# Two small tiles lengthened: where the operands of an encoder layer's products begin in a partition

## The chip, the core and the metric

The kernel runs on one core of one Trainium2 chip. The metric is the device time of one execution in microseconds (us), the median of several runs.

## What is computed

One layer of a bidirectional encoder, 256 tokens of 2048 features in float32: a half-step SwiGLU, a mixer with four neighbourhood heads and twelve dilated heads over one q/k/v projection, a second half-step SwiGLU, and a gated per-layer embedding. Each sublayer stands between two RMS norms.

```python
f = _swiglu(_rmsnorm(h, ffn1_pre_g[i]), ffn1_w_gate[i], ffn1_w_up[i], ffn1_w_down[i])
h = h + 0.5 * _rmsnorm(f, ffn1_post_g[i])
m = _mixer(_rmsnorm(h, mix_pre_g[i]), w_qkv[i], na_rpb[i], out_g[i], w_o[i])
h = h + _rmsnorm(m, mix_post_g[i])
f = _swiglu(_rmsnorm(h, ffn2_pre_g[i]), ffn2_w_gate[i], ffn2_w_up[i], ffn2_w_down[i])
h = h + 0.5 * _rmsnorm(f, ffn2_post_g[i])
g = jax.nn.sigmoid(_rmsnorm(h, ple_pre_g[i]) @ w_ple_gate[i])
h = h + _rmsnorm(g * (p[i] @ w_ple_proj[i]), ple_post_g[i])
```

The weight matrices are 2048 x 5632 (gate and up of both SwiGLUs, and their transposed shape for down), 2048 x 6144 (q/k/v), 2048 x 2048 twice (output and embedding gate) and 256 x 2048 (embedding projection).

## The kernel before

**The products.** `product` (L89) multiplies the activations of both token tiles (128 tokens each) with a block of 512 columns of a weight matrix. A float32 operand is split into two float32r parts, high and low, and three matmuls (L114, L115, L116) stand for one: high by high, low by high, high by low. In each of them the activation tile, 128 x 128, is the stationary operand, which TensorE loads by a LDWEIGHTS of its own, and the weight tile, 128 x 512, is the moving one. A name in the profile such as `down<-wh,hid_h` reads: result, moving operand, stationary operand. With three matmuls for each weight tile of 128 x 512 and each of two token tiles, the whole layer has 8304 of these matmuls.

**Stationary operands.** The normalised input of a sublayer lies in the tiles `u_h` and `u_l` of the pool `acts`; gate, up, q, k, v and the embedding gate (`pg`) read them. The embedding's own input `p_h`, `p_l` lies in the pool `work` (`pp` reads it). The hidden values of a SwiGLU and the heads' outputs lie in `hid_h` and `hid_l`, in pools that are opened behind all others (`ffn1`, `mix`, `ffn2`); down and the output projection (`mo`) read them.

**Moving operands.** `load_pairs` (L61) brings four row tiles of a weight into `raw` (three buffers) by one DMA of the SP queue, ScalarE writes the high part `wh` (L74 or L79), VectorE the low part `wl` (L75 or L80), seven buffers of two row tiles each, all in the pool `wpool`.

**Other work of TensorE.** Between the products stand transposes (L150, L353, L406), the scores (L391) and the weighted sums (L412) of the attention, all in plain float32.

**Where tiles lie.** Pools take up a partition one behind the other, in the order in which they are opened (L43 to L49), and a tile's length in bytes is rounded up to a multiple of 32. `mhalf` (L57) is the exponent -0.5 of the norms' power; it lies in the first pool, `const`, ahead of `h`, `acts`, `wpool`, `gpool` and `work`. `r` (L135) is the norm's factor, one float a token, in 16 buffers of the pool `small`, which is the last of the pools opened at the start; `ffn1`, `mix` and `ffn2` begin behind it. The order of the instructions is that of the program's text.

Of the kernel before, what the change touches and what calls it, by code (L numbers as in the profile page):

```python
# [15 lines left out]
P = 128  # L16
# [9 lines left out]
EPS = 1e-6  # L26
# [5 lines left out]

@with_exitstack
def encoder_layer(ctx: ExitStack, tc: tile.TileContext, a: dict, out: bass.AP):
    """One layer, 256 tokens in two tiles of 128 partitions.

    A float32 operand of a large product is split exactly into two float32r parts (12 bits of
    significand each); high x high + low x high + high x low are accumulated in PSUM. The weights
    stream through once, as the moving operand, for both token tiles.
    """  # L40
    nc = tc.nc

    const = ctx.enter_context(tc.tile_pool(name="const", bufs=1))  # L43
# [7 lines left out]
    ps_tr = ctx.enter_context(tc.tile_pool(name="ps_tr", bufs=2, space=PSUM))  # L51
    ps_o = ctx.enter_context(tc.tile_pool(name="ps_o", bufs=2, space=PSUM))

# [1 line left out]
    ident = const.tile([P, P], F32, name="ident")  # L55
    make_identity(nc, ident)
    mhalf = const.tile([P, 8], F32, name="mhalf")  # L57
    nc.gpsimd.memset(mhalf, -0.5)

# [1 line left out]
    def load_pairs(w, r0, nk, c0, g):  # L61
        """Split parts of w[r0 : r0 + nk * 128, c0 : c0 + 512], two row tiles at a time; with g,
        of the rows times the gain of their feature."""
        pairs = []
        for k0 in range(0, nk, 4):
            n = min(4, nk - k0)
            raw = wpool.tile([P, 4, NB], F32, name="raw", bufs=3)
            rows_ = w[r0 + k0 * P : r0 + (k0 + n) * P, c0 : c0 + NB]
            raw_loads.append(nc.sync.dma_start(raw[:, :n], rows_.rearrange("(k p) n -> p k n", p=P)))
            for j in range(0, n, 2):  # L70
                wh = wpool.tile([P, 2, NB], F32R, name="wh", bufs=7)
                wl = wpool.tile([P, 2, NB], F32R, name="wl", bufs=7)
                if g is None:
                    nc.scalar.copy(wh, raw[:, j : j + 2])  # L74
                    nc.vector.tensor_tensor(wl, raw[:, j : j + 2], wh.bitcast(F32), op=ALU.subtract)  # L75
                else:
                    for i in range(min(2, n - j)):
                        k = r0 // P + k0 + j + i
                        nc.scalar.activation(wh[:, i], raw[:, j + i], AF.Copy, scale=g[:, k : k + 1])  # L79
                        nc.vector.scalar_tensor_tensor(  # L80
                            wl[:, i], raw[:, j + i], g[:, k : k + 1], wh[:, i].bitcast(F32),
                            op0=ALU.mult, op1=ALU.subtract,
                        )
                pairs.append((wh, wl))
        return pairs
# [3 lines left out]
    def product(  # L89
        acc, lhs, w, r0, c0, g=None, first=True, last=True, steps=None, ahead=None, mid=None, jobs=True  # L90
    ):
        """acc[t] += lhs.T @ w[r0 : r0 + len(lhs) * 128, c0 : c0 + 512] for both token tiles.

        lhs[k] is (high, low), each [128, 256]. The row tiles of w are taken in steps (of SUPER
        at the most), each for one token tile and then the other, so that the first is done ahead
        of the second. ahead() comes before each step; with jobs, what waits in later comes behind
        the first; mid() comes where MID row tiles are left, of the second token tile.
        """
        nk = len(lhs)
        s0 = 0  # L100
        for n in steps or [nk % SUPER] * (nk % SUPER > 0) + [SUPER] * (nk // SUPER):
            if ahead is not None:
                ahead(s0)
            pairs = load_pairs(w, r0 + s0 * P, n, c0, g)
            for t in range(NT):
                tok = slice(t * P, (t + 1) * P)
                for k in range(n):
                    if mid is not None and t == NT - 1 and s0 + n == nk and k == n - MID:
                        mid()
                    wh, wl = pairs[k // 2]  # L110
                    xh, xl = lhs[s0 + k]
                    lead = first and s0 + k == 0
                    tail = last and s0 + k == nk - 1
                    nc.tensor.matmul(acc[t], xh[:, tok], wh[:, k % 2], start=lead, stop=False)  # L114
                    nc.tensor.matmul(acc[t], xl[:, tok], wh[:, k % 2], start=False, stop=False)  # L115
                    nc.tensor.matmul(acc[t], xh[:, tok], wl[:, k % 2], start=False, stop=tail)  # L116
            s0 += n
            if jobs:
                for job in later:
                    job()  # L120
                later.clear()
# [2 lines left out]
        return [ps_acc.tile([P, NB], F32, name=f"{name}{t}", tag="acc") for t in range(NT)]  # L124

    def gain(g, c0, name):
        """g[c0 : c0 + 512] in every partition."""
        t = gpool.tile([P, NB], F32, name=name, tag="gain")
        nc.sync.dma_start(t, bass.AP(tensor=g.tensor, offset=g.offset + c0, ap=[[0, P], [1, NB]]))
        return t  # L130

    def rsqrt_mean(v, n, scale):
        """v holds n partial sums of squares a token; 1 / (scale * sqrt(mean + EPS))."""
        m = small.tile([P, 1], F32, name="m")
        r = small.tile([P, 1], F32, name="r", bufs=16)  # L135
        c = scale * scale
        nc.vector.tensor_reduce(m, v, axis=AX.X, op=ALU.add)
        nc.gpsimd.tensor_scalar(m, m, c / n, c * EPS, op0=ALU.mult, op1=ALU.add)
# [5 lines left out]
        nc.scalar.activation(sq, x, AF.Square, accum_out=acc_col)  # L144

    def transposed_split(x, hi, lo, t):
        """x [128 tokens, 512] -> hi, lo [128, 4, 256], their columns of token tile t."""
        tr = ps_tr.tile([P, KB, P], F32, name="tr", tag="tr")
        for k in range(KB):
            nc.tensor.transpose(tr[:, k], x[:, k * P : (k + 1) * P], ident)  # L150
# [9 lines left out]
    def rows(blocks):  # L160
        return [(hi[:, k], lo[:, k]) for hi, lo in blocks for k in range(KB)]

# [1 line left out]
    h = resid.tile([P, NT, D], F32, name="h")  # L164

    # Gains of the features that go into a product, which are in the partitions of the weights:
    # of the four sublayers' inputs, and of the heads.
    row_g = const.tile([P, 5, D // P], F32, name="row_g")
    nc.sync.dma_start(row_g, a["row_gT"].rearrange("p (i k) -> p i k", i=5))

    # First input, from x with features in the partitions: loaded two row tiles at a time, between
    # those of the first weights.
    xT = a["xT"].rearrange("(k p) s -> p k s", p=P)
    x_blocks = [new_split(acts, "u", D // NB) for _ in range(D // NB)]

# [20 lines left out]
        return rsqrt_mean(ss, D, 1.0)  # L196

    def residual(fg, ssf, scale, blocks, rs):
        """h += fg / (scale * rms), transposed and split into blocks; and its pre-norm factor a
        token, which is applied behind the product and worked out behind its first part. A  # L200
        generator that stops after each half of a token tile; the first half needs fg[0] only."""
        blocks += [new_split(acts, "u", D // NB) for _ in range(D // NB)]
        r = []
        for b0 in range(0, D // NB, 2):
# [72 lines left out]
                down_out(1)  # L277
            f0 += ng

# [1 line left out]
    with tc.tile_pool(name="ffn1", bufs=2) as pool:  # L281
        f = pool.tile([P, NT, D], F32, name="f", bufs=1)
        ssf, u_blocks, u_rs = square_sums(), [], []
# [5 lines left out]
        list(res)  # L289
    rs = u_rs  # L290

# [1 line left out]
    mix = ctx.enter_context(ExitStack())  # L293
    pool = mix.enter_context(tc.tile_pool(name="mix", bufs=1))
    with ExitStack() as att:
        mconst = att.enter_context(tc.tile_pool(name="mconst", bufs=1))
        attn = att.enter_context(tc.tile_pool(name="attn", bufs=1))

        # Additive bias, queries in the partitions: [128, query tile, (head,) 256 keys].
        dil_bias = mconst.tile([P, NT, S], F32, name="dil_bias")  # L300
        nc.sync.dma_start(dil_bias, a["dil_bias"].rearrange("(t p) k -> p t k", p=P))
        na_mask = attn.tile([P, NT, S], F32, name="na_mask", tag="y", bufs=2)
        nc.sync.dma_start(na_mask, a["na_mask"].rearrange("(t p) k -> p t k", p=P))
        # In the place of the last heads' output.
        na_bias = [
            pool.tile([P, KB, S], F32, name="na_bias", tag=f"hid_{x}", bufs=4) for x in "hl"
        ]
        # Row q - k of the position bias: loaded with each grid row's queries in reverse, where it
        # is a window that moves by one a partition, and put in order by a permutation.
        flip = mconst.tile([P, P], F32, name="flip")  # L310
        nc.sync.dma_start(flip, a["flip"])
        rpb = a["rpb_pad"]
# [31 lines left out]
        later.append(query_factor)  # L344

        def heads_transposed(acc, fac, rotate, name):
            """[128, 4 heads, 256 tokens] of a projection, scaled and rotated."""
            xT_ = attn.tile([P, KB, S], F32, name=name)

            def turn(y, t):  # L350
# [27 lines left out]
            return xT_  # L378

        def attend(qT, kT, v, bias, o_split):  # L380
            """Four heads of softmax(q k + bias) v, normalised a head, transposed and split."""
            for t in range(NT):
                tok = slice(t * P, (t + 1) * P)
                o = ps_o.tile([P, KB, HD], F32, name="o")
# [50 lines left out]
        for g in range(4):  # L435
# [14 lines left out]
                nc.scalar.activation(v[:, t], acc[t], AF.Copy, scale=rs[t])  # L450
            o_split = new_split(pool, "hid", 4)
            if g == 0:
                bias = lambda t, hh: na_bias[t][:, hh]  # noqa: E731
            else:
                bias = lambda t, hh: dil_bias[:, t]  # noqa: E731
            attend(qT, kT, v, bias, o_split)
            o_blocks.append(o_split)

    # Output projection: the first two column blocks start on the heads that are done.
    lhs = rows(o_blocks)  # L460
    pool2 = mix.enter_context(tc.tile_pool(name="mix_f", bufs=1))
    f = pool2.tile([P, NT, D], F32, name="f")
# [25 lines left out]
    list(res)  # L488
    mix.close()

# [1 line left out]
    ffn2 = ctx.enter_context(ExitStack())  # L492
    f_pool = ffn2.enter_context(tc.tile_pool(name="f2", bufs=1, side="right"))
    p_h = work.tile([P, PLE // P, S], F32R, name="p_h", tag="hg")
# [11 lines left out]
            a["ffn2_w_gate"], a["ffn2_w_up"], a["ffn2_w_down"], a["ffn2_post_g"],  # L506
        )

# [1 line left out]
    pool = ctx.enter_context(tc.tile_pool(name="ple", bufs=1))  # L510
    p_rows = [(p_h[:, k], p_l[:, k]) for k in range(PLE // P)]
    pp = []
# [33 lines left out]


def _shape_constants():
    """Tables that depend on the shapes alone."""
    import numpy as np  # L550

    inv = np.float32(10000.0) ** (-np.arange(0, HD, 2, dtype=np.float32) / np.float32(HD))
# [56 lines left out]
```

## Time and profile before

| | |
|---|---|
| three runs, median (lowest to highest) | 2007.77 us (2007.38 to 2007.98) |
| profiled execution, first to last instruction | 2005.5 us |
| granted TensorE clock, mean | 0.998 |
| PE (matmul) busy | 1987.0 us, 99% |
| weight loads busy | 1630.2 us, 81% |
| VectorE busy | 1158.1 us, 58% |
| ScalarE busy | 1050.5 us, 52% |
| read from HBM | 373.40 MB, 187 GB/s |

The profile gives the profiled execution's span alone; the median of the runs is 2.3 us above it, which is what lies around the first and last instruction. Matmuls are pipelined: one lasts longer in its row than the distance to the start of the next, so the distance between starts, called the pitch here, is what a matmul costs in a dense stretch.

### The profile page before, as it was taken

Reading aid. Unit: us, or ns where it says so; the run is one execution under the profiler, and the core shown is the slowest. Engines: PE = TensorE matmul, PEld = TensorE weight load, DVE = VectorE, ACT = ScalarE, POOL = GpSimd, SP = SyncE. Lnnn points to the kernel's source line nnn. Section 1 sums busy time; section 2 is a strip of 40 time slices with the busy share of each in tenths; the row PEclk is TensorE's granted clock in tenths of the full one; section 3 lists DMA queues with packets and bytes.
Section 4 is the critical chain, followed back from the end, with each engine's and each line's share of the span. In section 5 each row is a group of like instructions: output and inputs, shape, how many; then the busy total and the mean of one; then the engine's idle time right before and its main releaser. Section 6 shows DMA issues by size and latency. Waiting matters only on the chain.

```text
span 2005.5 us, 23482 instructions
## 1 busy us (share of the span) xinstructions
PE 1987.0 (99%) x8936; PEld 1630.2 (81%) x8936; DVE 1158.1 (58%) x1659; ACT 1050.5 (52%) x1613; POOL 25.4 (1%) x47
## 2 busy tenths in 40 slices
PE   8999999999999999999999999999999999999998
PEld 7888888888888877888888788888888888888886
DVE  6755355655465566566565575654465645565664
ACT  7654455543455455655555564544454534453663
POOL 0000000000000000000000000000000000000000
PEclk9999999999999999999999999999999999999999
DMA  8755555555555557353454555555555555555562
GB/s 300 248 182 196 181 192 186 194 183 190 188 197 181 196 178 222 136 202 135 167 170 166 184 193 195 188 191 175 203 182 196 186 192 177 201 182 201 165 215 104
DMA packets 194561, 377.02 MB, mean 188 GB/s; under 512 B 10768, under 2 KB 13968, under 8 KB 194192
## 3 DMA queue, kind: packets, MB, share of 16 engines
q1 hardware_dynamic: 194448, 375.52, 54.7%
q8 instruction: 70, 1.15, 0.2%
q14 instruction: 43, 0.35, 0.0%
HBM read 373.40 MB, written 2.10 MB: 187 GB/s over the span
## 4 chain that ended last, share of the span: by engine, by line
PE 98%; DVE 1%; DMA 0%; issue 0%; POOL 0%; SPq 0%; ACT 0%; DVEq 0%; POOLq 0%; ACTq 0%
PE down L116 8%; PE down L115 8%; PE down L114 8%; PE up L116 8%; PE gate L116 8%; PE gate L115 8%; PE up L115 8%; PE gate L114 8%; PE up L114 8%; PE tr L150 2%; PE v L116 1%; PE pg L115 1%; PE k L116 1%; PE k L115 1%; PE v L115 1%; PE pg L114 1%
## 5 line engine op out<-in xcount | busy, mean ns | idle before, releaser
L79 ACT ACTIVATE wh<-raw,row_g 128x512 fp32r<-128x512 f32 x1024 | 686.9, 718 | 455.7 <-PE up L115 184.2
L80 DVE SCALAR_TENSOR_TENSOR wl<-raw,row_g,wh 128x512 fp32r<-128x512 f32 x1024 | 709.8, 748 | 334.6 <-ACT wh L79 334.5
L75 DVE TENSOR_TENSOR wl<-raw,wh 128x1024 fp32r<-128x1024 f32 x180 | 220.5, 1225 | 176.4 <-ACT wh L74 172.1
L74 ACT CAST wh<-raw 128x1024 fp32r<-128x1024 f32 x180 | 189.4, 1052 | 223.1 <-PE down L115 178.3
L114 PE MATMUL gate<-wh,u_h 128*128 128x512 f32 x704 | 276.6, 393 | 5.9 <-ACT wh L79 5.9
L114 PE MATMUL down<-wh,hid_h 128*128 128x512 f32 x704 | 279.0, 396 | 0.0
L116 PE MATMUL down<-wl,hid_h 128*128 128x512 f32 x704 | 278.6, 396 | 0.0
L115 PE MATMUL down<-wh,hid_l 128*128 128x512 f32 x704 | 278.4, 395 | 0.0
L116 PE MATMUL gate<-wl,u_h 128*128 128x512 f32 x704 | 275.5, 391 | 0.0
L115 PE MATMUL gate<-wh,u_l 128*128 128x512 f32 x704 | 275.4, 391 | 0.0
L116 PE MATMUL up<-wl,u_h 128*128 128x512 f32 x704 | 274.0, 389 | 0.0
L114 PE MATMUL up<-wh,u_h 128*128 128x512 f32 x704 | 273.9, 389 | 0.0
L115 PE MATMUL up<-wh,u_l 128*128 128x512 f32 x704 | 273.9, 389 | 0.0
L114 PEld LDWEIGHTS gate<-wh,u_h 128*128 128x128 f32 x704 | 132.9, 189 | 33.1 <-ACT wh L79 5.8
L116 PEld LDWEIGHTS down<-wl,hid_h 128*128 128x128 f32 x704 | 132.4, 188 | 31.8
L115 PEld LDWEIGHTS down<-wh,hid_l 128*128 128x128 f32 x704 | 132.4, 188 | 31.6
L114 PEld LDWEIGHTS down<-wh,hid_h 128*128 128x128 f32 x704 | 132.4, 188 | 31.4
L116 PEld LDWEIGHTS gate<-wl,u_h 128*128 128x128 f32 x704 | 132.6, 188 | 27.9 <-DVE wl L80 0.3
L115 PEld LDWEIGHTS gate<-wh,u_l 128*128 128x128 f32 x704 | 132.8, 189 | 27.4
L116 PEld LDWEIGHTS up<-wl,u_h 128*128 128x128 f32 x704 | 132.1, 188 | 27.9 <-DVE wl L80 0.3
L115 PEld LDWEIGHTS up<-wh,u_l 128*128 128x128 f32 x704 | 132.1, 188 | 27.4
L114 PEld LDWEIGHTS up<-wh,u_h 128*128 128x128 f32 x704 | 132.1, 188 | 27.4
(122 smaller groups left out, 1815.7 us busy)
## 6 DMA issues: line engine op xcount, KB each, us to landing
raw<-in_ffn_w_up SPq DMA_DIRECT2D x88, 1024.0 KB, 5.2
raw<-in_ffn_w_down SPq DMA_DIRECT2D x88, 1024.0 KB, 5.1
raw<-in_ffn_w_gate SPq DMA_DIRECT2D x84, 1024.0 KB, 5.3
raw<-in_w_qkv SPq DMA_DIRECT2D x48, 1024.0 KB, 5.2
raw<-in_w_o SPq DMA_DIRECT2D x16, 1024.0 KB, 5.1
raw<-in_w_ple_gate SPq DMA_DIRECT2D x16, 1024.0 KB, 5.1
raw<-in_ffn_w_gate SPq DMA_DIRECT2D x7, 512.0 KB, 5.3
xb<-in_xT SPq DMA_DIRECT2D x8, 256.0 KB, 4.3
```

Of the source, the lines that this page charges most:

```text
L74: nc.scalar.copy(wh, raw[:, j : j + 2])
L75: nc.vector.tensor_tensor(wl, raw[:, j : j + 2], wh.bitcast(F32), op=ALU.subtract)
L79: nc.scalar.activation(wh[:, i], raw[:, j + i], AF.Copy, scale=g[:, k : k + 1])
L80: nc.vector.scalar_tensor_tensor(wl[:, i], raw[:, j + i], g[:, k : k + 1], wh[:, i].bitcast(F32), op0=ALU.mult, op1=ALU.subtract,)
L114: nc.tensor.matmul(acc[t], xh[:, tok], wh[:, k % 2], start=lead, stop=False)
L115: nc.tensor.matmul(acc[t], xl[:, tok], wh[:, k % 2], start=False, stop=False)
L116: nc.tensor.matmul(acc[t], xh[:, tok], wl[:, k % 2], start=False, stop=tail)
L150: nc.tensor.transpose(tr[:, k], x[:, k * P : (k + 1) * P], ident)
```

## The change

`mhalf` gets 16 columns in place of 8, and `r` 30 buffers in place of 16. The first moves all that lies behind it by 32 bytes; the second moves what lies behind `small` by 448 bytes more. The added columns and buffers are otherwise as the old ones: the fill of `mhalf` is one instruction of the same kind, only the first columns are read, and `r` goes round 30 buffers. Comments and docstrings are taken out as well, with their lines left empty. On each engine the instructions stand in the same order as before, and their number is the same.

```diff
     ident = const.tile([P, P], F32, name="ident")
     make_identity(nc, ident)
-    mhalf = const.tile([P, 8], F32, name="mhalf")
+    mhalf = const.tile([P, 16], F32, name="mhalf")
     nc.gpsimd.memset(mhalf, -0.5)
...
         m = small.tile([P, 1], F32, name="m")
-        r = small.tile([P, 1], F32, name="r", bufs=16)
+        r = small.tile([P, 1], F32, name="r", bufs=30)
```

The first byte of the tiles in each partition, as the built programs place them (buffers of one name lie 2048 or 4096 bytes apart, and the slices that a matmul takes are multiples of 512 bytes further, so the remainder is that of every operand):

| tile | part | before, bytes (remainder by 512) | with the change |
|---|---|---|---|
| `wh`, `wl` | moving, all products | 91104, 119776 (480) | 91136, 119808 (0) |
| `u_h`, `u_l` | stationary: gate, up, q, k, v, pg | 33760, 50144 (480) | 33792, 50176 (0) |
| `p_h`, `p_l` | stationary: pp | 154592, 156640 (480) | 154624, 156672 (0) |
| `hid_h`, `hid_l` of ffn1 | stationary: down | 191008, 207392 (32) | 191488, 207872 (0) |
| `hid_h`, `hid_l` of mix | stationary: mo | 168480, 184864 (32) | 168960, 185344 (0) |
| `hid_h`, `hid_l` of ffn2 | stationary: down | 178720, 195104 (32) | 179200, 195584 (0) |
| `ident` | moving, transposes | 16512 (128) | 16512 (128) |
| `kT`, `v` | moving, attention | 214048, 218144 (32) | 214528, 218624 (0) |

## Rows read from the trace of the kernel before

**Rows 1.** The page's head, engine rows, granted clock; then the view of cores.
```profile
span 2005.5 us, 23482 instructions
PE 1987.0 (99%) x8936; PEld 1630.2 (81%) x8936; DVE 1158.1 (58%) x1659; ACT 1050.5 (52%) x1613; POOL 25.4 (1%) x47
PEclk9999999999999999999999999999999999999999
core 0: 2005.5 us, clock 0.998
```

**Rows 2.** The page's chain that ended last; then TensorE's longest wait in the waits.
```profile
PE 98%; DVE 1%; DMA 0%; issue 0%; POOL 0%; SPq 0%; ACT 0%; DVEq 0%; POOLq 0%; ACTq 0%
...
PE gate L114 <- ACT wh L79: 5.9, 1, 5.9
```

**Rows 3.** Groups by line and shape: operands, count, busy us, mean ns of one, idle before.
```profile
L114 PE MATMUL down<-wh,hid_h 128*128 128x512 f32 x704 | 279.0, 396 | 0.0
L114 PE MATMUL gate<-wh,u_h 128*128 128x512 f32 x704 | 276.6, 393 | 5.9 <-ACT wh L79 5.9
L114 PE MATMUL up<-wh,u_h 128*128 128x512 f32 x704 | 273.9, 389 | 0.0
L114 PE MATMUL q<-wh,u_h 128*128 128x512 f32 x128 | 52.2, 408 | 0.0
L114 PE MATMUL mo<-wh,hid_h 128*128 128x512 f32 x128 | 51.1, 399 | 0.0
L114 PE MATMUL pp<-wh,p_h 128*128 128x512 f32 x16 | 6.2, 390 | 0.0
```

**Rows 4.** Timeline of TensorE, 125 to 145 us (start us, us): 90 matmuls, stationary `u`.
```profile
124.61 0.39 PE L116 MATMUL up<-wl,u_h 128*128 128x512 f32 x1
...
144.79 0.39 PE L115 MATMUL gate<-wh,u_l 128*128 128x512 f32 x1
```

**Rows 5.** Timeline of TensorE, 210 to 230 us: 87 matmuls, stationary `hid` of ffn1.
```profile
209.81 0.40 PE L115 MATMUL down<-wh,hid_l 128*128 128x512 f32 x1
...
229.87 0.40 PE L114 MATMUL down<-wh,hid_h 128*128 128x512 f32 x1
```

**Rows 6.** Timeline, 1070 to 1080 us: 44 matmuls; 1902 to 1906 us: 17 matmuls.
```profile
1069.80 0.40 PE L116 MATMUL mo<-wl,hid_h 128*128 128x512 f32 x1
...
1079.84 0.39 PE L114 MATMUL mo<-wh,hid_h 128*128 128x512 f32 x1
...
1901.69 0.39 PE L115 MATMUL pp<-wh,p_l 128*128 128x512 f32 x1
...
1905.32 0.39 PE L116 MATMUL pp<-wl,p_h 128*128 128x512 f32 x1
```

**Rows 7.** Plain float32: timeline at 107 and 828 us, then groups by line.
```profile
107.60 1.03 PE L150 MATMUL tr<-ident,hm 128*128 128x128 f32 x8
...
828.31 0.60 PE L391 MATMUL sc<-kT,qT 128*128 128x256 f32 x2
...
L150 PE MATMUL tr<-ident,hm 128*128 128x128 f32 x176 | 22.8, 272 | 0.0
...
L391 PE MATMUL sc<-kT,qT 128*128 128x256 f32 x64 | 18.4, 380 | 0.0
```

**Rows 8.** Groups by line, 1157 to 1158.9 us: products ahead of a wait.
```profile
L114 PE MATMUL gate<-wh,u_h 128*128 128x512 f32 x2 | 0.8, 388 | 0.0
L150 PE MATMUL tr<-ident,h 128*128 128x128 f32 x2 | 0.4, 286 | 0.9 <-DVE h L210 0.9
```

**Rows 9.** Timeline behind eight transposes, 108 to 110 us.
```profile
108.71 0.40 PE L115 MATMUL gate<-wh,u_l 128*128 128x512 f32 x1
108.94 0.40 PE L116 MATMUL gate<-wl,u_h 128*128 128x512 f32 x1
109.18 0.39 PE L114 MATMUL gate<-wh,u_h 128*128 128x512 f32 x1
```

**Rows 10.** Busy time by stretch (PE, loads, DVE, ACT, POOL, clock, DMA share, GB/s); largest DMAs.
```profile
125.00:145.00 20.00, 20.00 (x90) 16.55 (x89) 12.37 (x18) 10.70 (x16) 0.00 (x0) 1.00 0.54 180
210.00:230.00 20.00, 20.00 (x87) 16.11 (x86) 7.75 (x7) 7.43 (x9) 0.00 (x0) 1.00 0.50 182
...
9.00:20.00 11.00, 11.00 (x45) 8.98 (x44) 8.22 (x12) 7.49 (x13) 0.00 (x0) 1.00 0.93 315
...
raw<-in_ffn_w_up SPq DMA_DIRECT2D x88, 1024.0 KB, 5.2
```

**Rows 11.** Timeline at 826 us; groups by line: the attention's short matmuls and their loads.
```profile
826.41 1.10 PE L412 MATMUL o<-v,pts 128*128 128x128 f32 x8
...
L412 PE MATMUL o<-v,pts 128*128 128x128 f32 x128 | 17.9, 282 | 0.0
...
L412 PEld LDWEIGHTS o<-v,pts 128*128 128x128 f32 x128 | 15.5, 191 | 3.7 <-ACT pts L408 3.7
```

## Prediction, made before the change was run

> **What bounds the kernel now.** I read the head of the page and the engine rows first: TensorE's matmuls are busy for 1987.0 of 2005.5 us, and the granted clock is 0.998 on average, which of the two levels, 1.2 and 2.4 GHz, is the upper one [rows 1]. The chain of work that ended last lies for 98% on TensorE, and its longest single wait is 5.9 us for the first weights [rows 2]. So only two things can move the time: how many matmuls there are, and how far apart they start. The groups by line give the number: gate and up 704 times three, q, k, v and the embedding gate 128 times three each, pp 16 times three, together 5808 with a stationary operand in `u` or `p`; down 704 times three and mo 128 times three, together 2496 with one in `hid` (k, v and pg have the counts of q) [rows 3]. All 8304 have the same shape, 128x512.
>
> The timeline gives the pitch, the distance from start to start. With `u` stationary 89 steps take 144.79 - 124.61 = 20.18 us, 0.2267 us each [rows 4]. With `hid` stationary 86 steps take 20.06 us, 0.2333 us each [rows 5]. The output projection, whose weights are prepared as gate's are and whose stationary operand is `hid`, has 10.04 / 43 = 0.2335; the embedding projection, whose weights are prepared as down's are and whose stationary operand lies at remainder 480, has 3.63 / 16 = 0.2269 [rows 6]. So neither ScalarE's and VectorE's way of preparing weights nor the kind of product sets the pitch. What goes with it is the remainder by 512 of the stationary operand's first byte: 480 gives 0.2267, 32 gives 0.2333, with the moving operand at 480 in both.
>
> In cycles of 2.4 GHz (0.4167 ns) that is 544 and 560 for 512 columns, 32 and 48 more than one column a cycle would take. The plain float32 matmuls have no such surplus: eight transposes of 128 columns last 1.03 us in all and one of them 0.272, so the pitch is (1.03 - 0.272) / 7 = 0.1083 us, 260 cycles, two a column and 4 over; two scores of 256 columns give 0.60 - 0.38 = 0.22 us, 528 cycles, two a column and at most 16 over, although their operands lie at remainder 32 too [rows 7]. A stream at two cycles a column thus pays next to nothing for where it lies; one at a cycle a column pays 32 to 48 cycles for something.
>
> **The change, part by part.** The longer `mhalf` fills eight more columns in one instruction on POOL in the first microseconds, and more buffers of `r` can only take waits away; neither touches the chain [rows 2], and I cost both at nothing. Were POOL's fill late, it would have to outlast the 5.9 us wait for the first weights to matter. No instruction, DMA or wait is added or moved. What is left is the addresses: the operands of all 8304 matmuls now begin at remainder 0.
>
> What that does to the pitch is shown by no row, so I bound it. Nearest on the low side is one column a cycle and nothing else, 512 cycles, 0.2133 us; on the high side the pitches that the trace has, 0.2267 and 0.2333. I take 0.2155, 512 cycles and some 5 over, the surplus of the transposes being 4 [rows 7], for two reasons. First, 544 is 17 times 32: a moving operand of 2048 bytes that begins 96 bytes into a block of 128 touches 17 such blocks, and one that begins at 0 touches 16; if TensorE takes whole blocks at 32 columns each, the pitch is exactly the 544 that is measured, and aligned it is 512 plus the surplus between two matmuls. That is a reading of one number, not something a row shows. Second, the surplus of 32 cycles is there where no weight load runs beside the matmul: ahead of a wait of 0.9 us, gate matmuls last 388 ns, one of them with no load behind it, against 389 in the dense stretch [rows 3, 8]; the scores, also 512 cycles long, last 380 [rows 7]. So some 8 ns belong to the matmul's own reading. That the rest of `hid`'s 560 goes as well is less sure; it is a collision of the load with the stream that needs the two at different remainders, which they no longer have.
>
> The sum, against the profiled execution: 5808 x (0.2267 - 0.2155) = 65.0 us, and 2496 x (0.2333 - 0.2155) = 44.4 us, together 109.4 of 2005.5, which gives 1896.1; the median of the runs is 2.3 above the span, so **1898 us**. With 0.2133 it would be 1880, with 528 cycles (0.2200: one block of 16 columns left over, the most that the scores show) 38.9 + 33.2 = 72.1 less, 1936. These are the bounds of this case.
>
> The Trainium skill, "TensorE: Matmul & The Clock Gate", section "Wait — 56ns, not 53.3ns?", gives 215.7 ns from start to start for 512 columns at the upper clock; with it the sum would be an estimate of 107.8 us, and the time 1900. No run here shows a product at that pitch.
>
> What would be late next? At 0.2155 the 24 matmuls of a 1 MB load take 5.17 us, 203 GB/s; the stretch from 9 to 20 us moves 315 GB/s, and the loads are issued three buffers ahead, so DMA, at a share of 0.54, does not take over. VectorE has 12.37 of 20 us in the gate and up stretch, which becomes 65% [rows 10]. Weight loads of 191 ns follow each other at a pitch of (1.10 - 0.282) / 7 = 0.117 us in the attention [rows 11], so a load of 0.19 us in 0.2155 is no bound either.
>
> **The rivals.**
>
> *Only the distance counts.* The load of the next stationary operand and the moving stream read at the same time and get in each other's way, by an amount that depends on their distance by 512. For it: between [rows 4] and [rows 5, 6] only the stationary operand's place differs; and just behind transposes the gate product, at unchanged addresses, runs at 0.23 and 0.24 before it settles [rows 9], so timing plays a part. Against it: the matmuls without a load beside them are as long [rows 8]. Then `u` stays at 0.2267, since its distance is 0 now as then, and `hid` joins it: 2496 x 0.0066 = 16.5 us, 1989.0 of span, 1991 us. Between this and the forecast lies a mixed case, with part of the 32 cycles gone.
>
> *Places do not count.* The 32 cycles belong to the float32r form at a cycle a column, and the 16 more to something else that `hid` has, such as lying in the last third of the partition, where it still lies. Then the change does nothing: 2008 us. Against it speaks that one remainder after the other sorts all products without exception [rows 4 to 6]. The Trainium skill, "SBUF — State Buffer", section "Door 1: The DMA port swizzle", states that SBUF has lines of 16 bytes and that reads pay for crossing into another line; by that rule remainders of 32 and 480, both multiples of 16, are as good as 0, and the time would stay at 2008. No run here shows yet whether 16 bytes suffice; the trace has no operand at another remainder.
>
> *Everything in one place: slower.* With all operands at remainder 0, the load, the stream and the writes of ScalarE and VectorE into `wh` and `wl` begin at the same position of a bank more often. The place is the gate, up, q, k, v and pg products. Priced by the worst settled pitch that the trace has, 0.2333, they would cost 5808 x 0.0066 = 38.3 us more, with `hid` unchanged: 2046 us. It decides from the point where the mean pitch is above today's (5808 x 0.2267 + 2496 x 0.2333) / 8304 = 0.2287. For it: the passing 0.23 to 0.24 of [rows 9] shows that operands with equal remainders can collide. Against it: gate's operands have equal remainders now, 480 and 480, and settle at the lower pitch [rows 4].
>
> **How the numbers follow.** Forecast with its bounds, 1880 to 1936: 0.43. The mixed case, 1936 to 1985: 0.07. Only the distance, about 1991: 0.24. No effect: 0.12. Slower: 0.14. A measurement of this kernel can tell about 0.2%, 4 us, from no change. The likeliest case alone reaches from 1880 to 1936. The range has to take in the distance case, and the unchanged case, to leave out no more than 2 in 10: 1880 to 2010 holds 0.86 with the slower case left out. Faster by over 0.2% are the first three cases, 0.74; within 0.2%, 0.12; slower, 0.14.
>
> **What would show it.** In the timeline of the changed kernel the steps in the up product (124 to 145 us before) should be 0.215 to 0.216 us, and in the down product the same: right. 0.2267 in both: only the distance counts. The two as before: places do not count. Above 0.2287 on average: the slower case. The gate matmul ahead of a wait should last about 380 ns, not 388. The time is wrong, with the pitch right, if TensorE's rows begin to show waits for `wh` or `wl`, or if the stretch by stretch DMA share rises towards its 0.93 of the first 20 us. The forecast falls if the granted clock drops below 0.99 over a stretch of products, since every price here is taken at the upper level.

## The result, and the profile after

The changed kernel takes 1990.51 us (median of 4 runs, 1989.66 to 1991.08), the kernel before 2007.58 beside it (4 runs, 2006.92 to 2007.98): a ratio of 0.9915, 95% interval 0.9901 to 0.9929. It is faster by 17 us, not by the 109 of the forecast. The time lies on the value of the first rival, 1991; the stated range, 1880 to 2010, holds it only because it was drawn to take in that rival and no change as well, and the forecast's own bounds, 1880 to 1936, do not.

The page's head and engine rows of the changed kernel, then its chain that ended last:

```profile
span 1988.8 us, 23482 instructions
...
PE 1969.9 (99%) x8936; PEld 1629.7 (82%) x8936; DVE 1155.9 (58%) x1659; ACT 1050.2 (53%) x1613; POOL 25.4 (1%) x47
...
PE 96%; DMA 1%; DVE 1%; ACT 1%; issue 0%; POOL 0%; SPq 0%; DVEq 0%; POOLq 0%; ACTq 0%
```

The span is 16.7 us shorter than in [rows 1] and TensorE is as full as it was. The number of matmuls is the same, so the pitch must have moved. The timeline of TensorE at 125 to 145 us (90 matmuls, `u` stationary) and at 210 to 230 us (90 matmuls, `hid` stationary), start and length in us, first and last row of each:

```profile
124.65 0.39 PE L115 MATMUL up<-wh,u_l 128*128 128x512 f32 x1
...
144.82 0.39 PE L114 MATMUL gate<-wh,u_h 128*128 128x512 f32 x1
...
209.62 0.39 PE L116 MATMUL down<-wl,hid_h 128*128 128x512 f32 x1
...
229.80 0.39 PE L115 MATMUL down<-wh,hid_l 128*128 128x512 f32 x1
```

Up takes 20.17 / 89 = 0.2266 us, what it took in [rows 4]; down takes 20.18 / 89 = 0.2267 in place of the 0.2333 of [rows 5]. So `hid` has joined `u`, and nothing has gone below 0.2267. With 2496 matmuls that read `hid`, 2496 x (0.2333 - 0.2267) = 16.5 us: the whole of the gain. The groups by line say the same in their mean durations: down had 396 ns in [rows 3] and now has 390, beside up's 389:

```profile
L114 PE MATMUL down<-wh,hid_h 128*128 128x512 f32 x704 | 274.5, 390 | 0.0
...
L114 PE MATMUL up<-wh,u_h 128*128 128x512 f32 x704 | 274.0, 389 | 0.0
```

And a gate matmul that has no load behind it, because the next transpose waits for VectorE, is as long as in [rows 8] (groups by line, 1147.4 to 1149.0 us; the matmul ahead of the 1.00 us wait is one of the two of the row):

```profile
L114 PE MATMUL gate<-wh,u_h 128*128 128x512 f32 x2 | 0.8, 388 | 0.0
```

The forecast wanted 380 here.

### The profile page after: what moved, and what is told of

Same layout as the page of the kernel before. It is cut to its first block, busy times and chain, and to the rows that moved or that the text cites. A ratio compares the mean times of both kernels' runs of the same rounds, so it can differ in the third digit from the quotient of the medians.

```text
span 1988.8 us, 23482 instructions
## 1 busy us (share of the span) xinstructions
PE 1969.9 (99%) x8936; PEld 1629.7 (82%) x8936; DVE 1155.9 (58%) x1659; ACT 1050.2 (53%) x1613; POOL 25.4 (1%) x47
## 4 chain that ended last, share of the span: by engine, by line
PE 96%; DMA 1%; DVE 1%; ACT 1%; issue 0%; POOL 0%; SPq 0%; DVEq 0%; POOLq 0%; ACTq 0%
PE down L116 8%; PE down L114 8%; PE down L115 8%; PE up L116 8%; PE up L114 8%; PE up L115 8%; PE gate L116 8%; PE gate L115 8%; PE gate L114 8%; PE tr L150 2%; PE q L116 1%; PE q L115 1%; PE q L114 1%; PE pg L116 1%; PE pg L114 1%; PE k L116 1%
## 5 line engine op out<-in xcount | busy, mean ns | idle before, releaser
L114 PE MATMUL down<-wh,hid_h 128*128 128x512 f32 x704 | 274.5, 390 | 0.0
L116 PE MATMUL down<-wl,hid_h 128*128 128x512 f32 x704 | 274.1, 389 | 0.0
L115 PE MATMUL down<-wh,hid_l 128*128 128x512 f32 x704 | 273.9, 389 | 0.0
```

## The experiments

Two things were to be told apart: what took down from 0.2333 to 0.2267, and why nothing fell to 0.2155. On the first, theory A is the rival that was right, that the distance between the stationary and the moving operand sets the pitch; rival B is that an operand's own place does. Distance is the first byte of the stationary tile less that of the moving one, by 512. Edits are shown against the kernel before; `...` stands for lines left out. From the map of distances onward every kernel also has the two lines of the whole change, which are not shown again.

**The longer `r` alone.** All operands stay off the multiples of 64, at remainder 480.

```diff
-        r = small.tile([P, 1], F32, name="r", bufs=16)
+        r = small.tile([P, 1], F32, name="r", bufs=30)
```

> Only the longer r: moving and all stationary operands at remainder 480, so at distance 0 with none of them at a multiple of 64. Theory A (the distance between the stationary and the moving operand sets the pitch): down and mo fall from 0.2333 to 0.2267 us as with the whole change, about 1991 us, or 1 to 2 us more where the products take longer to settle behind transposes. Rival B (hid gains because it now begins at a multiple of 512 itself): down and mo stay at 0.2333, about 2008 us.

Measured: 1990.82 us (5 runs), ratio to before 0.9916, interval 0.9903 to 0.9930. The timeline of the down product, 215 to 235 us, 90 matmuls:

```profile
214.65 0.39 PE L116 MATMUL down<-wl,hid_h 128*128 128x512 f32 x1
...
234.82 0.39 PE L115 MATMUL down<-wh,hid_l 128*128 128x512 f32 x1
```

20.17 / 89 = 0.2266. This half of the change gives the whole gain; multiples of 512 are not needed.

**The longer `mhalf` alone.** `u` and the moving operands at 0, `hid` at 64.

```diff
-    mhalf = const.tile([P, 8], F32, name="mhalf")
+    mhalf = const.tile([P, 16], F32, name="mhalf")
```

> Only the longer mhalf: moving operands and u at remainder 0, hid at 64. Theory A: down and mo stay at 0.2333, the rest at 0.2267, about 2007 us. Rival B: hid at a multiple of 64 is enough, down and mo fall to 0.2267, about 1991 us. Rival C (gate, up and the rest gain from remainder 0): below 0.2267 there; the whole change has shown 0.2267, so not expected.

Measured: 2006.72 us (10 runs), ratio 0.9996, interval 0.9987 to 1.0005. Down, 215 to 235 us, 88 matmuls, then up, 90:

```profile
214.60 0.40 PE L114 MATMUL down<-wh,hid_h 128*128 128x512 f32 x1
...
234.91 0.39 PE L114 MATMUL down<-wh,hid_h 128*128 128x512 f32 x1
...
124.79 0.39 PE L116 MATMUL up<-wl,u_h 128*128 128x512 f32 x1
...
144.97 0.39 PE L115 MATMUL gate<-wh,u_l 128*128 128x512 f32 x1
```

0.2334 and 0.2267, both as before. Putting `u`, `wh` and `wl` at multiples of 512 changes nothing that these runs can measure. Theory A holds in both halves, rival B in neither.

**A map of distances.** Three kernels with the whole change and unused pad tiles at the head of the pools that hold `hid`, of 32, 96 and 128 bytes, then 192, 256 and 448, then 160, 224 and 320 (the first is shown).

```diff
     with tc.tile_pool(name="ffn1", bufs=2) as pool:
+        pool.tile([P, 8], F32, name="pad1", bufs=1)
...
     pool = mix.enter_context(tc.tile_pool(name="mix", bufs=1))
+    pool.tile([P, 24], F32, name="padm")
...
     with tc.tile_pool(name="ffn2", bufs=2) as pool:
+        pool.tile([P, 32], F32, name="pad2", bufs=1)
```

> The whole change, with unused pad tiles that put the hidden tiles of ffn1 at distance 32, those of the mixer at 96 and those of ffn2 at 128 from the moving operand. Theory A: each stage has a pitch of its own, between 0.2133 and 0.2360; if the pattern repeats every 128 bytes, ffn2's down has 0.2267 and the others 0.23 or more; if every 512, all three differ from 0.2267. All at 0.2333 would give 2007 us. Rival B (only multiples of 512, or of 64, are good): 128 alone is good by 64, none by 512.

> The same with distances 192 (ffn1), 256 (mixer) and 448 (ffn2), the last being 64 the other way round. Theory A with a repeat of 128: 256 gives 0.2267, 192 and 448 give 0.2333 as 64 does. With a repeat of 512: three pitches of their own, and 448 may differ from 64, since a load that lies ahead of the stream is not a load behind it. Between 1985 and 2010 us.

> The whole change, with the hidden tiles of ffn1 at distance 160, of the mixer at 224 and of ffn2 at 320 from the moving operand. A repeat every 256 bytes, as 256 (0.2267) and the equal pitches at 192 and 448 (0.2289) have it, says that 320 gives what 64 gives, 0.2333; 160 lies between 128 (0.2324) and 192 (0.2289), about 0.231; 224 between 192 and 256, 0.2267 to 0.2289, and below 0.2267 if 0 is not the best distance. No repeat: 320 gives anything else. About 2000 us.

Measured: 2006.59, 1996.74 and 2006.25 us, one run each. The pitch of each stage, first to last row of a stretch of the timeline (215 to 235, 1070 to 1078, 1370 to 1390 us), with the kernels above at 0 and 64:

| distance | stage | steps | pitch, us |
|---|---|---|---|
| 0 | ffn1 down, whole change | 89 | 0.2267 |
| 32 | ffn1 down | 86 | 0.2334 |
| 64 | ffn1 down, `mhalf` alone | 87 | 0.2334 |
| 96 | mo | 35 | 0.2343 |
| 128 | ffn2 down | 86 | 0.2324 |
| 160 | ffn1 down | 86 | 0.2334 |
| 192 | ffn1 down | 88 | 0.2289 |
| 224 | mo | 35 | 0.2334 |
| 256 | mo | 36 | 0.2267 |
| 320 | ffn2 down | 86 | 0.2334 |
| 448 | ffn2 down | 88 | 0.2290 |

The rows of 256, of the output projection:

```profile
1069.74 0.39 PE L115 MATMUL mo<-wh,hid_l 128*128 128x512 f32 x1
...
1077.90 0.39 PE L115 MATMUL mo<-wh,hid_l 128*128 128x512 f32 x1
```

8.16 / 36 = 0.2267. Three pairs that differ by 256 agree: 0 and 256, 64 and 320, 192 and 448. So the pattern repeats every 256 bytes as far as these pairs go, and of the eight distances in steps of 32 only 0 is free of the extra. The guess for 320 was right; those for 160 (0.231) and 224 (0.2267 to 0.2289) were wrong, so the pattern is not a smooth one, and why 192 costs a third of the others is not explained here.

**`u` moved off instead.** The whole change and an unused tile ahead of the weights' tiles.

```diff
     # ---- constants ----
+    wpool.tile([P, 48], F32, name="padw", bufs=1)
...
```

> The whole change with an unused tile of 192 bytes ahead of the weights' tiles: the moving operands and all that lies behind them are at remainder 192, u alone stays at 0. So hid and p keep distance 0, and u gets -192, which is 64 if the pattern repeats every 256 bytes. Theory A with that repeat: down, mo and pp at 0.2267 although none of them lies at a multiple of 512 or 256; gate, up, q, k, v and pg, 5760 matmuls, at 0.2333, 38 us more than the change, about 2029 us. Rival (it is hid's own place that matters, or a multiple of 512): down and mo away from 0.2267, gate and the rest, whose stationary operand has not moved, at 0.2267; about 2007 us.

Measured: 2026.16 us (4 runs), ratio to before 1.0093, interval 1.0076 to 1.0110. Up (125 to 145 us, 88 matmuls) and down (213 to 233 us, 90):

```profile
124.66 0.39 PE L115 MATMUL up<-wh,u_h 128*128 128x512 f32 x1
...
144.96 0.39 PE L115 MATMUL gate<-wh,u_h 128*128 128x512 f32 x1
...
212.61 0.39 PE L115 MATMUL down<-wh,hid_h 128*128 128x512 f32 x1
...
232.79 0.39 PE L117 MATMUL down<-wl,hid_h 128*128 128x512 f32 x1
```

20.30 / 87 = 0.2333 for up, whose stationary operand has not moved and is now at distance -192, 64 by 256; and 0.2267 for down. The rule is not about `hid`: what loses is whichever product has its two operands at the wrong distance. Expected 38 us above the change, measured 35.7. The slower rival's price, 38.3, was thus a real one; its mechanism, equal remainders colliding, is the reverse of what happens.

**Where the 32 cycles are.** The second question, with three more kernels on the whole change. First, loads that read a quarter of the bytes; in every product the rows of 96 of a tile's 128 tokens miss all but the first and last matmul. A pad of 64 bytes at the head of `ffn1` is part of it.

```diff
...
-                    nc.tensor.matmul(acc[t], xl[:, tok], wh[:, k % 2], start=False, stop=False)
...
+                    part = slice(t * P, t * P + 32)
...
+                    nc.tensor.matmul(acc[t][:32], xl[:, part], wh[:, k % 2], start=False, stop=False)
...
```

> The whole change, but all matmuls of a product except its first and its last take 32 of a tile's 128 tokens as stationary operand, so that a load reads a quarter of the bytes; 96 of 128 rows of each result miss most of their sum. ffn1's hidden tiles are put at distance 64, all others at 0. Theory L (the 32 cycles over 512 are what the load's reading takes from the stream): with a quarter of the load the surplus falls to some 8 to 13 cycles, a pitch of 0.2165 to 0.2190, and ffn1's down, at distance 64, falls from 0.2333 as well; about 1910 us. Theory F (the 32 cycles belong to the moving float32r operand itself, as the prediction had it but without a way to align them away): gate and up stay at 0.2267 and only ffn1's down falls, to 0.2267 or a little more; about 1991 us.

Measured: 2027.55 us, one run: both theories fell. A load's row (125 to 145 us) and the up product's timeline, 88 matmuls:

```profile
L118 PEld LDWEIGHTS up<-wh,u_h 128*32 128x32 f32 x26 | 2.8, 109 | 3.1
...
124.69 0.39 PE L118 MATMUL up<-wh,u_h 128*32 128x512 f32 x1
...
144.82 0.39 PE L118 MATMUL gate<-wh,u_h 128*32 128x512 f32 x1
```

The loads last 109 ns in place of 188, and the pitch is 20.13 / 87 = 0.2314, longer than with whole loads. ffn1's down, at distance 64, has 0.2315 (88 steps), so the distance makes no difference here. The surplus does not shrink with what a load reads. Since the edit also leaves 96 of the 128 stationary columns, and so 96 rows of the result, out of each matmul, the run does not say what makes the pitch longer.

Second, both parts in bfloat16 (the results then carry bfloat16 parts in place of float32r ones).

```diff
-F32R = mybir.dt.float32r
+F32R = mybir.dt.bfloat16
...
-                    nc.vector.tensor_tensor(wl, raw[:, j : j + 2], wh.bitcast(F32), op=ALU.subtract)
+                    nc.vector.tensor_tensor(wl, raw[:, j : j + 2], wh, op=ALU.subtract)
```

> The whole change with both parts of every product in bfloat16 in place of float32r, so that load and stream have half the bytes for the same 512 columns (the result has bfloat16's accuracy in the two parts). Under theory L and theory F alike the stream then has reading time to spare: pitch 0.2155 by the prediction's floor, 8304 x 0.0112 = 93 us less, about 1898 us. Rival: the surplus comes with every load whatever its bytes: 0.2267, 1991 us.

Measured: 1903.51 us, one run. A group by line, and up's timeline, 71 matmuls:

```profile
L114 PE MATMUL up<-wh,u_h 128*128 128x512 bf16 x704 | 266.8, 379 | 0.9 <-ACT wh L79 0.9
...
124.72 0.38 PE L114 MATMUL up<-wh,u_h 128*128 128x512 bf16 x1
...
139.83 0.38 PE L115 MATMUL gate<-wh,u_l 128*128 128x512 bf16 x1
```

15.11 / 70 = 0.2159 us, 518 cycles: one column a cycle and 6 over. This is the pitch that the prediction wanted from alignment, and bfloat16 operands give it. The edit halves the bytes of the stream and of the load (a load lasts 98 ns in place of 188) and changes the number format, all at once, so this run alone does not say which of them does it.

Third, one product of each kind with altered operands. In ffn1's gate every column of the stationary operand is one token's, in its up every column of the moving operand is one weight column, its down is cut into halves of 256 columns, and ffn2's low hidden tiles lie 64 bytes off.

```diff
...
+                    if w is a["ffn1_w_gate"]:
+                        xh, xl = (v[:, :1].broadcast_to([P, P]) for v in (xh, xl))
+                    if w is a["ffn1_w_up"]:
+                        mh, ml = (v[:, :1].broadcast_to([P, NB]) for v in (mh, ml))
+                    wid = NB // 2 if w is a["ffn1_w_down"] else NB
+                    for c in range(0, NB, wid):
...
```

> The whole change, with one product of each kind altered, so that each stage shows one thing; most results are not the layer's. ffn1's gate takes one token's column for all 128 stationary columns (a load that reads a single element per partition), ffn1's up takes one weight column for all 512 moving ones (a stream that reads a single element), ffn1's down runs each matmul as two of 256 columns (same columns, twice the loads), and in ffn2 the low hidden tiles are put 64 bytes further than the high ones. Theory F (the 32 cycles are the rate at which a float32r stream is read): gate 0.2267, up 0.2155, down 0.1133 for each half, and 1990 us or less. Theory G (32 cycles with every matmul that has a load beside it, whatever it reads): gate and up 0.2267, down 0.1200 for each half, ffn1's down 14 us longer in all. Theory L (what the load reads): gate below 0.2267; short loads made the pitch longer, so hardly expected. ffn2's down: if a load disturbs the stream that runs while it reads, the pitch of the matmuls that run beside a load of the low tile (the first of each three) is the longer, and the mean is 0.2267 to 0.2333.

Measured: 2003.43 us, one run. Timelines: gate at 96 to 106 us (46 matmuls) and at 141 to 149 us (36), up at 121 to 132 us (52), down at 210 to 220 us (86), then five consecutive starts of ffn2's down and its groups by line, 1375 to 1395 us:

```profile
95.64 0.40 PE L122 MATMUL gate<-wh,u_h 128*128 128x512 f32 x1
...
105.94 0.40 PE L122 MATMUL gate<-wh,u_h 128*128 128x512 f32 x1
...
140.81 0.39 PE L122 MATMUL gate<-wh,u_h 128*128 128x512 f32 x1
...
148.91 0.40 PE L124 MATMUL gate<-wl,u_h 128*128 128x512 f32 x1
...
120.78 0.38 PE L123 MATMUL up<-wh,u_l 128*128 128x512 f32 x1
...
131.83 0.38 PE L123 MATMUL up<-wh,u_l 128*128 128x512 f32 x1
...
209.74 0.28 PE L122 MATMUL down<-wh,hid_h 128*128 128x256 f32 x1
...
219.94 0.28 PE L123 MATMUL down<-wh,hid_l 128*128 128x256 f32 x1
```

```profile
1380.85 0.39 PE L122 MATMUL down<-wh,hid_h 128*128 128x512 f32 x1
1381.08 0.40 PE L123 MATMUL down<-wh,hid_l 128*128 128x512 f32 x1
1381.32 0.39 PE L124 MATMUL down<-wl,hid_h 128*128 128x512 f32 x1
1381.55 0.39 PE L122 MATMUL down<-wh,hid_h 128*128 128x512 f32 x1
1381.77 0.40 PE L123 MATMUL down<-wh,hid_l 128*128 128x512 f32 x1
...
L123 PE MATMUL down<-wh,hid_l 128*128 128x512 f32 x30 | 11.9, 397 | 0.0
L122 PE MATMUL down<-wh,hid_h 128*128 128x512 f32 x30 | 11.8, 392 | 0.0
L124 PE MATMUL down<-wl,hid_h 128*128 128x512 f32 x29 | 11.3, 389 | 0.0
```

- Down in halves: 10.20 / 85 = 0.1200 us, 288 cycles for 256 columns. The surplus is again 32 cycles, as for 512 columns, so it comes once with a matmul and not with each column; theory F, which wanted 0.1133, falls, and theory G's number is met. A rival is that loads cannot follow each other faster than 0.1200 us. Against it, the plain float32 transposes, which have a load each, start every 0.1083 us [rows 7]; no dense stretch here has float32r loads closer than 0.1200.
- Up with a stream that reads one element: 11.05 / 51 = 0.2167 us, 520 cycles. Loads and columns are as many as ever and all but 8 of the 32 cycles are gone (of the three steps the one of the matmul with `u_l` is the longer, 0.220 against 0.215 us), so theory G, "whatever it reads", falls too: the cost goes with what the stream reads.
- Gate with a load that reads one element: 10.30 / 45 = 0.2289 at 96 to 106 us, and 8.10 / 35 = 0.2314 at 141 to 149 us. As with short loads, taking reads away from the load does not lower the pitch.
- ffn2's down, the low tile off by 64: of the three steps from 1380.85 the second is the longer, 0.24 against 0.23, and over all its steps in ffn2 the mean is 0.2359 us, against 0.2290 and 0.2284 for the first and third. The groups by line have the same order. Expected was the first, which runs while the low tile is loaded. So, as the rows have their starts, the extra shows in the matmul whose own stationary operand is off, not in the one beside whose stream that operand is loaded.

Together: with float32r operands each matmul pays 32 cycles once, at either width; bfloat16 operands, or a stream that stays on one element, take most or all of it away; a shorter load does not. What happens in these cycles, and how a stationary operand at another distance than 0 by 256 adds 5 to 18 more, is not settled by these runs.

## Why the prediction was right or wrong

- **What bounds the kernel: right.** The pitch of 8304 matmuls is the time. Every run here is told by it to a few us: the changed kernel by 16.5 of 16.7 us of span.
- **What sorts the pitch: half read.** The remainder of the stationary operand did go with the pitch. But the moving operand lay at 480 in all products, so remainder and distance could not be told apart in the rows, and the text passed from one to the other. The two halves of the change and the kernel with `u` moved off show that it is the distance, by 256.
- **The failed step: "a moving operand of 2048 bytes that begins 96 bytes into a block of 128 touches 17 such blocks".** It was to turn 544 cycles into 517 once the operand begins at 0, and carried the term 5808 x (0.2267 - 0.2155) = 65.0 us on the products with `u` and about 28 of the 44.4 us on those with `hid`. At remainder 0 the pitch is 0.2266: neither of these came, and of the 109.4 us only the 16.5 did that `hid` had over `u`. So the blocks are not what costs. The text called it "a reading of one number, not something a row shows", and that number, 544 = 17 x 32, is as well 512 and 32. The kernel with down in halves tells the two apart: 256 columns that begin at remainder 0 fill eight blocks of 128 bytes, 256 cycles and some 5 over by the prediction's rule, and take 288. In the changed kernel the 32 cycles are still there, and they go with float32r operands and with what the stream reads; why is open.
- **The second reason did not carry.** The matmul ahead of a wait is as long as one in the stream, 388 ns before and after. But the ends of matmuls are modelled in the profile, and in the kernel before a q matmul at 770 us, with `u` at distance 0 and no load behind it, has 397, so single rows of this kind show little. And "belongs to the matmul's own reading" does not say "goes with alignment". What [rows 3] and [rows 7] set apart was float32r at a cycle a column from plain float32 at two, and this stood there under the rival "places do not count", as a part of the float32r form.
- **The rest of `hid`'s surplus: right in what it depends on, its mechanism not shown.** It went when the two operands came to the same position, at the price of the first rival, 16.5 us. That it is "a collision of the load with the stream" beside it no run shows. With the low tile alone off, the longer step is that of the matmul whose own stationary operand is off. Single rows point the same way, for what they are worth: the last down matmul ahead of a wait, with no load behind it, lasts 397 ns before (742 us) and 388 in the changed kernel (735 us); at 1892 us before it is 390. Groups by line of the first two:

```profile
L115 PE MATMUL down<-wh,hid_l 128*128 128x512 f32 x1 | 0.4, 397 | 0.0
...
L115 PE MATMUL down<-wh,hid_l 128*128 128x512 f32 x1 | 0.4, 388 | 0.0
```

- **The rivals.** "Only the distance counts", with 0.24, gave 1991 and was met by 1990.51; its condition and its price hold, its mechanism, the load of the next operand against the stream, is as little shown. Its counter-argument, that matmuls without a load are as long, bears on the 32 cycles that all products share, not on the extra that `hid` had beyond them. The likeliest case should have been this one: it needed only what [rows 4 to 6] show, while the forecast needed a pitch that no row had.
- **The page on SBUF: half right.** The Trainium skill, "SBUF — State Buffer", section "Door 1: The DMA port swizzle", has lines of 16 bytes as the grain. For an operand's own place that agrees: 480 and 0 give 0.2266 both. For two operands it is not enough: all distances of the map are multiples of 16, and they give 0.2267 to 0.2343.
- **The page on TensorE's reads.** The Trainium skill, "TensorE: Matmul & The Clock Gate", section "Part 2: What happens when you issue a matmul", holds that loading the next tile's weights takes no read bandwidth from the running matmul, the two having ports of their own. The runs agree in so far as a load that reads less gives nothing back (0.2314 with short loads). They also show that the stationary operand is not without effect: between the kernel before and the longer `r` alone its place is all that moves in down, and the pitch goes from 0.2333 to 0.2266.

## What to carry to other kernels

Where TensorE is full, measure the pitch of each product in the timeline and compare it between products of the same shape; a difference that follows the operands' places is worth a pad tile, and here 448 bytes gave 17 us while 192 in the wrong place cost 36. In a kernel like this one, place stationary and moving float32r operands at the same position by 256 bytes; no run here shows that their absolute place matters. A surplus that all products share should not be counted as a gain until one product has been seen without it.

## What the runs showed that was not expected

- The extra of a wrong distance repeats every 256 bytes and does not grow with the distance: 0.2334 us at 32, 64, 160 and 224, 0.2343 at 96, 0.2324 at 128, 0.2289 at 192.
- Less reading by the load went with a longer pitch: 0.2314 with 32 columns, 0.2289 to 0.2314 with a single element, against 0.2267 with a whole load at distance 0.
- At distance 0 a float32r matmul costs 32 cycles over its columns at 512 and at 256 columns alike, so cutting a product into narrower matmuls costs twice: 2 x 0.1200 against 0.2267 us.
- Bfloat16 parts of the same shape run at 0.2159 us, and the kernel with them at 1903.51 us, with coarser parts.
